# Two layers of a hybrid diffusion trunk: the beginning redone, a fourth load buffer, modulation sums closed two steps later

## Chip, cores and metric

One core of a Trainium2 chip. The time is the device time of one execution in microseconds; the kernel before was run three times: 1830.18, 1832.28 and 1832.47 us, median 1832.28. A separate execution was profiled: 1824.12 us, with a span of 1822.3 us from the first to the last instruction.

## The reference, cut to what matters

256 latent tokens `x` and 256 context tokens `ctx`, each of 1024 features, go through two layers. Every sub-layer normalises its input, scales and shifts it by vectors that a linear map makes from a condition (`c` for latent tokens, `c_ctx` for context tokens), and gates its output.

```python
def sandwich_in(x, mods, idx, g_pre):
    shift, scale = mods[3 * idx], mods[3 * idx + 1]
    return rms_norm(x, g_pre) * (1 + scale) + shift

def swiglu(h, w1, w2):
    a, b = jnp.split(h @ w1, 2, axis=-1)
    return (jax.nn.silu(a) * b) @ w2

    silu_c, silu_cc = jax.nn.silu(c), jax.nn.silu(c_ctx)
    for layer in range(DEPTH):
        m_lat = split(silu_c @ w_ada[layer] + b_ada[layer], 9)
        m_ctx = split(silu_cc @ w_ada[layer] + b_ada[layer], 9)
        # half-step SwiGLU, token mixing (three groups of heads), half-step SwiGLU
```

`w_ada` is 1024 x 9216 per layer, `ffn_w1` 1024 x 5632 and `ffn_w2` 2816 x 1024 per feed-forward. All is in 32-bit floating point.

## The kernel before

Activations lie feature-major: HH and HL hold, for each of the 8 tiles of 128 features, the high and the low part of 512 token columns (context 0 to 255, latent 256 to 511). Each product of 32-bit numbers is three matmuls, high by high, high by low and low by high. Weights come as units of mostly 512 KB: SyncE loads one into a buffer of the ring `raws` (three buffers), ScalarE casts it into the high part of a slot (line 186), VectorE subtracts to get the low part (line 191), and the buffer is free again. A unit for the modulation vectors of later sub-layers (`ada_v`, lines 446 to 491) isn't split: VectorE multiplies its rows by the condition and adds them up in SX (lines 464, 466), four units to a half of a block; then a step `red` sums over the partitions with four matmuls and copies the result into `rows` on ScalarE (line 474), and a step `fin` transposes `rows` (line 482) and adds biases (`mod_done`), or, for a gate, works on rows of GROW and writes them out (`gate_done`). For gates, `gate_rows` reads bias and norm rows into GROW (lines 432, 433) ahead of the four units.

The order of the work is written as lists of steps. `schedule` merges a main list with side steps that have due points (`spread` puts the modulation steps evenly into a feed-forward body); `run` walks the merged list and, before each step, issues loads as long as the buffer that the load needs has been freed, and splits as slots come free. The framework below then orders each engine's instructions by readiness in its own model of time, so an instruction may stand earlier in its engine's queue than its step. Every engine works its queue in order, SyncE's loads included.

The beginning. `start` asks for x, the two conditions (element by element into `csrc`, lines 1169 and 1170), constants and ctx. `x_stat` normalises the tokens of a group into GTB (lines 1186, 1191); `load_x` transposes all 8 feature tiles of the group and copies them from PSUM banks to YB (lines 1201, 1202). The first sub-layer's shift and scale are made tile by tile: `ada_k` multiplies the condition `sc` by two 512 KB blocks of `w_ada` (32 small matmuls), copies the sums into `rows` (line 1216), transposes (line 1221) and adds bias and gain. The blocks of tile 0 lie in `raws`, the others in three own buffers, the two halves of GTB and a part of SX, which are free only when the tokens have left GTB. `pre_one` scales and shifts one tile of one group (lines 1234 to 1236) into HH and HL, and `first_k` runs that tile's 18 matmuls of 512 columns for the first three pairs of hidden tiles, while later tiles are still being made. The order is pre_one(k), ada_k(k+2), first_k(k).

The buffer R holds split weights (XS slots), hidden activations (U), and in the mixing stage attention buffers, at overlapping addresses.

Of the kernel before, what the change touches and what calls it, by code (L numbers as in the profile page):

```python
# [16 lines left out]
P = 128  # L17
D = 1024
# [61 lines left out]
def hybrid_trunk(ctx: ExitStack, tc, x, c, ctx_in, c_ctx, w_ada, b_ada, norm_g, ffn_w1, ffn_w2, w_in, w_out,  # L80
# [36 lines left out]
    raws = [tile(f"raw{i}", [1024]) for i in range(3)]  # L117
# [10 lines left out]
    JUNK = tile("junk", [D], mybir.dt.bfloat16)  # L128
# [8 lines left out]
    U_HI = [R[:, i * 1024 : i * 1024 + T] for i in range(NU)]  # L137
    U_LO = [R[:, i * 1024 + T : (i + 1) * 1024] for i in range(NU)]
    XS = [R[:, 9216 + i * 2048 : 9216 + (i + 1) * 2048].rearrange("p (a n) -> p a n", a=2) for i in range(5)]
# [25 lines left out]
    class Unit:  # L165


        def __init__(self, src, split=True, slots=(0, 1, 2), lo=V):
            self.src, self.split, self.slots, self.lo_eng = src, split, slots, lo
            self.nk, self.n = src.shape[0] // P, src.shape[1]  # L170
            self.first = self.last = self.own = self.own_prev = None
            self.after, self.hi_v, self.tail = -1, False, False
# [33 lines left out]
    class Step:  # L206


        def __init__(self, fn, units=(), dur=0.0, after=(), needs=(), low=False):
            self.fn, self.units, self.dur, self.after, self.needs = fn, list(units), dur, list(after), list(needs)  # L210
            self.low = low
# [46 lines left out]
    def run():  # L258
# [108 lines left out]
    csrc = tile("csrc", [KD, 2])  # L367
# [9 lines left out]
    def layer_consts(l):  # L377
        ng, ba = S1(), S1()
        nc.scalar.dma_start(out=ng[0:48, 0:P], in_=norm_g[l].rearrange("a (k p) -> (a k) p", p=P))
        nc.scalar.dma_start(out=ba[0:72, 0:P], in_=b_ada[l].rearrange("(k p) -> k p", p=P))  # L380
        pt = XB()
# [66 lines left out]
    def ada_v(l, *js):  # L448

        st = []  # L450
        for j in js:
            for h in range(2):
                box = {}
                if j % 3 == 2:
                    st.append(Step(lambda l=l, j=j, h=h: gate_rows(l, j, h)))
                for q in range(4):
                    u = Unit(w_ada[l, q * SEQ : (q + 1) * SEQ, j * D + h * T : j * D + (h + 1) * T], split=False)
# [32 lines left out]
                st += [Step(red, dur=0.43), Step(fin, dur=0.0 if j % 3 == 2 else 0.22)]  # L490
        return st
# [20 lines left out]
    def tok_end(g, t, o, partial):  # L512
# [3 lines left out]
        for hf, c_ in enumerate(HALVES):  # L516
            if partial:
                V.tensor_tensor(out=y[:, c_], in0=o[hf], in1=y[:, c_], op=ALU.add)
            S.activation(out=JUNK[:, :T], in_=y[:, c_] if partial else o[hf], func=AF.Square, scale=RMS, accum_out=st[:, hf : hf + 1])
# [3 lines left out]
        for hf, c_ in enumerate(HALVES):  # L523
            V.scalar_tensor_tensor(out=x[:, c_], in0=S2T[:, c_], scalar=r, in1=x[:, c_], op0=ALU.mult, op1=ALU.add)  # L524
            S.activation(out=JUNK[:, :T], in_=x[:, c_], func=AF.Square, scale=RMS, accum_out=st[:, 2 + hf : 3 + hf])
# [27 lines left out]
    def out_end(t, o):  # L553

        st, x, gy = SR(), X[:, 2 + t], (S2T, SX[:, :D])[t]
        for hf in range(2):
            S.activation(out=JUNK[:, :T], in_=o[hf], func=AF.Square, scale=RMS, accum_out=st[:, hf : hf + 1])
# [604 lines left out]
    def start():  # L1162
# [6 lines left out]
        nc.scalar.dma_start(out=csrc[:, :, 0], in_=c_ctx.rearrange("(k p) -> p k", p=P))  # L1169
        nc.scalar.dma_start(out=csrc[:, :, 1], in_=c.rearrange("o (k p) -> p (o k)", p=P))  # L1170
        nc.sync.dma_start(out=cst[:, 0 : 3 * P], in_=const[:, 0 : 3 * P])
        for t in range(2):
            nc.sync.dma_start(out=xs[CTXG][:, t], in_=ctx_in[0, t * P : (t + 1) * P])
        S.activation(out=sc[:, 0, 0:1], in_=eps, func=AF.Silu)

    start()
    BX = Ring(banks[0:4] + banks[6:8])

    def start_late():
        nc.sync.dma_start(out=cst[:, 3 * P :], in_=const[:, 3 * P :])  # L1180

    def x_stat(g):

        st = SR()
        for t in range(2):
            S.activation(out=JUNK, in_=xs[g][:, t], func=AF.Square, scale=RMS, accum_out=st[:, t : t + 1])
        if g == LAT:
            S.activation(out=sc[:, :, 0:2], in_=csrc, func=AF.Silu)
        for t in range(2):
# [3 lines left out]
    def by_feature(g, ks):  # L1193
        return YB.rearrange("p g n -> p (g n)").rearrange("p (k t) -> p k t", k=KD)[:, ks, GROUPS[g]]

    def load_x(g):
        for kk in range(0, KD, 2):
            pt = BX().rearrange("p (k t) -> p k t", k=2)
            for z in range(2):
                for t in range(2):  # L1200
                    nc.tensor.transpose(out=pt[:, z, t * P : (t + 1) * P], in_=GTB[:, t, (kk + z) * P : (kk + z + 1) * P], identity=ident)
            V.tensor_copy(out=by_feature(g, slice(kk, kk + 2)), in_=pt)
# [28 lines left out]
    def pre_one(k, g):  # L1231
        gs = GROUPS[g]
        t = S2()[:, :SEQ]
        V.tensor_scalar(out=t, in0=by_feature(g, k), scalar1=A[0][:, 0, k, g : g + 1], scalar2=MOD[0][:, k, g : g + 1], op0=ALU.mult, op1=ALU.add)
        S.copy(out=HH[:, k, gs], in_=t)
        V.tensor_tensor(out=HL[:, k, gs], in0=t, in1=HH[:, k, gs].bitcast(F32), op=ALU.subtract)
# [23 lines left out]
    both = (LAT, CTXG)  # L1260
# [8 lines left out]
    consts0 = Step(lambda: layer_consts(0))  # L1269
    lx = {g: Step(lambda g=g: load_x(g), dur=1.7) for g in both}  # L1270
    flat = [u for us in ada0[1:] for u in us]
    for i, u in enumerate(flat):
        u.own, u.own_prev = raw_u[i % 3], flat[i - 3] if i >= 3 else consts0 if i == 2 else lx[CTXG]
    rs = {g: Step(lambda g=g: x_stat(g), dur=0.43) for g in both}
    pre = {(k, g): Step(lambda k=k, g=g: pre_one(k, g)) for k in range(KD) for g in both}
# [82 lines left out]
```

## Time and profile before

| | |
|---|---|
| median of three runs | 1832.28 us |
| profiled execution | 1824.12 us, span 1822.3 us |
| TensorE matmul busy | 1750.3 us, 96% |
| TensorE weight load busy | 1452.9 us, 80% |
| VectorE, ScalarE, GpSimd busy | 1170.7, 714.8, 72.8 us |
| read from memory | 257.51 MB, 142 GB/s over the span |
| mean granted TensorE clock | 0.987 of full |

Busy shares are means over stages with different limits. A group's idle time says what its engine waited for just before it; matmuls are pipelined, so a busy TensorE is not one at its peak. PE is TensorE's matmul, PEld its weight load, DVE VectorE, ACT ScalarE, POOL GpSimd, SPq the queue of SyncE.

### The profile page before, as it was taken

How to read it: one execution, taken by the hardware profiler on the slowest of the kernel's cores; microseconds unless marked ns; L12 is line 12 of the kernel's file. 1: busy time of each engine (PE TensorE's matmuls, PEld its weight loads, DVE VectorE, ACT ScalarE, POOL GpSimd, SP SyncE). 2: the span in 40 equal slices, each digit the busy share in tenths (PEclk: the TensorE clock that was granted, in tenths of full speed). 3: DMA queues.
4: the chain of work that ended last, by engine and by line, in shares of the span. 5: the costliest groups of instructions: out<-in, count | busy, mean ns of one | idle time of the engine just before them, and what ended most of it. 6: DMA issues, size and time to landing. Idle time of an engine off the chain costs nothing.

```text
span 1822.3 us, 24374 instructions
## 1 busy us (share of the span) xinstructions
PE 1750.3 (96%) x9496; PEld 1452.9 (80%) x9496; DVE 1170.7 (64%) x1889; ACT 714.8 (39%) x1244; POOL 72.8 (4%) x128
## 2 busy tenths in 40 slices
PE   4999999999999999999999999999999999969998
PEld 3788777778977779878878798888887897859997
DVE  4756776667367875757758565666765737865553
ACT  3323222235267763323222442322223526654442
POOL 0000000001000400000000000000000100200000
PEclk8999999999999999999999999999999999979999
DMA  7836555554211152656545334645554431255662
GB/s 230 243 116 192 176 173 157 167 171 125 57 47 47 64 171 71 188 163 182 176 148 176 124 105 127 197 122 183 176 161 156 115 69 58 93 151 187 187 187 76
DMA packets 301187, 260.19 MB, mean 143 GB/s; under 512 B 18064, under 2 KB 246160, under 8 KB 301072
## 3 DMA queue, kind: packets, MB, share of 16 engines
q1 hardware_dynamic: 297216, 257.67, 46.5%
q8 instruction: 74, 1.21, 0.3%
q10 hardware_dynamic: 3856, 0.97, 0.2%
q14 instruction: 41, 0.34, 0.1%
HBM read 257.51 MB, written 1.10 MB: 142 GB/s over the span
## 4 chain that ended last, share of the span: by engine, by line
PE 65%; DMA 14%; DVE 12%; ACT 5%; issue 3%; POOL 1%; SPq 0%; ACTq 0%; DVEq 0%; POOLq 0%
PE bank L90 62%; DMA raw<-in_ffn_w_dram 10%; DVE sx L466 3%; DVE R L191 2%; ACT R L186 2%; DVE w L191 2%; DMA raw<-in_w_ada_dram 2%; ACT w L186 1%; DMA gtb<-in_w_ada_dram 1%; POOL sr L507 1%; PE bank L802 1%; PE bank L536 1%; DMA csrc<-in_c_dram 1%; DVE sx L464 0%; DVE X L524 0%
## 5 line engine op out<-in xcount | busy, mean ns | idle before, releaser
L90 PE MATMUL bank<-HH,R 128*128 128x512 f32 (+1 forms) x2028 | 531.7, 347 | 4.7 <-ACT R L186 2.5
L90 PE MATMUL bank<-HH,w 128*128 128x512 f32 (+1 forms) x1540 | 433.9, 359 | 0.4 <-DVE w L191 0.4
L90 PEld LDWEIGHTS bank<-HH,R 128*128 128x128 f32 x2028 | 356.3, 191 | 59.5 <-issue 7.2
L90 PE MATMUL bank<-R 128*128 128x512 f32 (+3 forms) x1632 | 364.1, 376 | 2.9 <-DVE YB L642 1.1
L90 PE MATMUL bank<-HL,R 128*128 128x512 f32 (+1 forms) x1014 | 349.5, 345 | 0.0
L90 PEld LDWEIGHTS bank<-R 128*128 128x128 f32 (+1 forms) x1632 | 278.5, 188 | 74.0 <-issue 9.7
L191 DVE TENSOR_TENSOR R<-raw,R 128x1024 fp32r<-128x1024 f32 (+1 forms) x177 | 214.7, 1216 | 173.5 <-ACT R L186 170.1
L466 DVE SCALAR_TENSOR_TENSOR sx<-raw,sc,sx 128x512 f32<-128x512 f32 x448 | 310.8, 745 | 21.8 <-DMA raw<-in_w_ada_dram 21.4
L186 ACT CAST R<-raw 128x1024 fp32r<-128x1024 f32 (+1 forms) x177 | 184.3, 1043 | 343.3 <-DMA raw<-in_ffn_w_dram 270.3
L90 PEld LDWEIGHTS bank<-HH,w 128*128 128x128 f32 x1540 | 274.1, 190 | 50.2 <-issue 12.0
L191 DVE TENSOR_TENSOR w<-raw,w 128x1024 fp32r<-128x1024 f32 (+1 forms) x153 | 187.5, 1226 | 161.8 <-ACT w L186 161.5
L90 PE MATMUL bank<-HL,w 128*128 128x512 f32 (+1 forms) x770 | 274.7, 357 | 0.0
L186 ACT CAST w<-raw 128x1024 fp32r<-128x1024 f32 (+1 forms) x153 | 159.9, 1046 | 279.8 <-DMA raw<-in_ffn_w_dram 199.6
L90 PE MATMUL bank<-w,R 128*128 128x512 f32 x960 | 236.0, 396 | 2.6 <-ACT R L1008 1.8
L90 PEld LDWEIGHTS bank<-w,R 128*128 128x128 f32 x960 | 178.1, 189 | 43.4 <-ACT R L1008 2.3
L90 PEld LDWEIGHTS bank<-HL,R 128*128 128x128 f32 x1014 | 193.3, 191 | 22.4 <-DVE HL L541 0.2
L90 PEld LDWEIGHTS bank<-HL,w 128*128 128x128 f32 x770 | 146.5, 190 | 20.6 <-issue 2.3
L591 DVE TENSOR_TENSOR sil<-sil,bank 128x512 f32<-128x512 f32 (+1 forms) x96 | 55.5, 578 | 77.9 <-PE bank L90 77.7
L593 ACT CAST R<-sil 128x512 fp32r<-128x512 f32 (+1 forms) x96 | 51.2, 533 | 135.0 <-DVE sil L591 135.0
L507 POOL TENSOR_TENSOR sr<-sr,eps 128x1 f32<-128x1 f32 x42 | 28.3, 674 | 1463.5 <-DVE sr L506 1444.5
L590 ACT ACTIVATE sil<-bank 128x512 f32<-128x512 f32 (+1 forms) x96 | 48.9, 510 | 90.7 <-PE bank L90 84.4
L360 DVE TENSOR_TENSOR R<-bank,R 128x512 fp32r<-128x512 f32 (+2 forms) x86 | 47.9, 561 | 33.8 <-ACT R L359 33.5
(145 smaller groups left out, 1211.8 us busy)
## 6 DMA issues: line engine op xcount, KB each, us to landing
raw<-in_ffn_w_dram SPq DMA_DIRECT2D x258, 512.0 KB
raw<-in_w_ada_dram SPq DMA_DIRECT2D x130, 512.0 KB
raw<-in_w_in_dram SPq DMA_DIRECT2D x40, 512.0 KB
raw<-in_w_out_dram SPq DMA_DIRECT2D x24, 512.0 KB
gtb<-in_w_ada_dram SPq DMA_DIRECT2D x10, 512.0 KB
gtb<-gate SPq DMA_DIRECT2D x10, 512.0 KB
raw<-in_ffn_w_dram SPq DMA_DIRECT2D x8, 384.0 KB
sx<-in_w_ada_dram SPq DMA_DIRECT2D x4, 512.0 KB
```

The source lines that it names most:

```text
L90: return nc.tensor.matmul(out=o, lhsT=l, rhs=r, start=start, stop=stop)
L186: ins = S.copy(out=self.hi, in_=self.raw)
L191: ins = self.lo_eng.tensor_tensor(out=self.lo, in0=self.raw, in1=self.hi.bitcast(F32), op=ALU.subtract)
L360: V.tensor_tensor(out=lo, in0=src, in1=hi.bitcast(F32), op=ALU.subtract)
L466: V.scalar_tensor_tensor(out=ACC[v], in0=u.raw[:, z, :], scalar=sv, in1=ACC[v], op0=ALU.mult, op1=ALU.add)
L507: G.tensor_tensor(out=a, in0=a, in1=mhalf, op=ALU.pow)
L536: nc.tensor.transpose(out=pt[:, z, t * P : (t + 1) * P], in_=y[:, t, k * P : (k + 1) * P], identity=ident)
L590: S.activation(out=sl[:, cs], in_=oa, func=AF.Silu)
L591: V.tensor_tensor(out=sl[:, cs], in0=sl[:, cs], in1=ob, op=ALU.mult)
L593: tab["hs"] = S.copy(out=uh[:, cs], in_=sl[:, cs])
L802: nc.tensor.transpose(out=b[:, n * P : (n + 1) * P], in_=e[:, n * P : (n + 1) * P], identity=ident)
```

## The change

The conditions are loaded as 16 rows of 128 values, put through Silu, transposed once and copied into `sc` (`conditions`); the norm gains and biases of layer 0 are asked for at the start into the buffers `sil`, as are the condition rows. The context tokens are asked for after the blocks of tile 0; the first rows of w1 wait for a mark behind that. `x_stat` writes normalised tokens to YB instead of GTB, in half-row statistics; `load_x` is gone, and `pre_k` transposes one feature tile of both groups into one bank, scales from the bank and casts and subtracts over 512 columns. GTB and the part of SX are free for modulation blocks from the start. `raws` has four buffers; `junk` is halved, `csrc` gone. XS and U have other addresses in R. In `ada_v` `gate_rows` stands behind two of the four load steps, and `take` puts the step `fin` of each half block behind the first two steps of the next one.

```diff
-    raws = [tile(f"raw{i}", [1024]) for i in range(3)]
+    raws = [tile(f"raw{i}", [1024]) for i in range(4)]
-    U_HI = [R[:, i * 1024 : i * 1024 + T] for i in range(NU)]
+    U_AT = [i * 1024 for i in range(8)] + [19456]
+    U_HI = [R[:, i : i + T] for i in U_AT]
-    XS = [R[:, 9216 + i * 2048 : 9216 + (i + 1) * 2048].rearrange("p (a n) -> p a n", a=2) for i in range(5)]
+    XS = [R[:, 8192 + i * 2048 : 8192 + (i + 1) * 2048].rearrange("p (a n) -> p a n", a=2) for i in range(5)]
...
         def can_load(i):
-            if nl >= len(seq):
+            if nl >= len(seq) or mark.get(seq[nl].gate, -1) > i:
                 return False
             if seq[nl].own is not None:
                 p = seq[nl].own_prev
-                return (p.last if isinstance(p, Unit) else prog.index(p)) < i
+                return p is None or p.last < i
...
-                if j % 3 == 2:
-                    st.append(Step(lambda l=l, j=j, h=h: gate_rows(l, j, h)))
                 for q in range(4):
+                    if q == 2 and j % 3 == 2:
+                        st.append(Step(lambda l=l, j=j, h=h: gate_rows(l, j, h)))
...
                 st += [Step(red, dur=0.43), Step(fin, dur=0.0 if j % 3 == 2 else 0.22)]
+                st[-1].fin = True
...
-        nc.scalar.dma_start(out=csrc[:, :, 0], in_=c_ctx.rearrange("(k p) -> p k", p=P))
-        nc.scalar.dma_start(out=csrc[:, :, 1], in_=c.rearrange("o (k p) -> p (o k)", p=P))
+        nc.scalar.dma_start(out=CROW[0:KD, 0:P], in_=c_ctx.rearrange("(k p) -> k p", p=P))
+        nc.scalar.dma_start(out=CROW[KD : 2 * KD, 0:P], in_=c.rearrange("o (k p) -> (o k) p", p=P))
+        consts_load(0, *CSRC)
...
+    def conditions():
+        S.activation(out=CROW[0 : 2 * KD], in_=CROW[0 : 2 * KD], func=AF.Silu)
+        pt = XB()
+        nc.tensor.transpose(out=pt[:, 0 : 2 * KD], in_=CROW[0 : 2 * KD], identity=ident[0 : 2 * KD, 0 : 2 * KD])
+        V.tensor_copy(out=sc[:, :, 0:2].rearrange("p k v -> p v k"), in_=pt[:, 0 : 2 * KD].rearrange("p (v k) -> p v k", v=2))
...
         for t in range(2):
-            root(st, t)
-            V.tensor_scalar(out=GTB[:, t], in0=xs[g][:, t], scalar1=st[:, t : t + 1], scalar2=None, op0=ALU.mult)
+            for hf, c_ in enumerate(HALVES):
+                S.activation(out=JUNK, in_=xs[g][:, t, c_], func=AF.Square, scale=RMS, accum_out=st[:, 2 * t + hf : 2 * t + hf + 1])
+            V.tensor_scalar(out=y_of(g)[:, t], in0=xs[g][:, t], scalar1=root(st, 2 * t, 2 * t + 1), scalar2=None, op0=ALU.mult)
...
+    def pre_k(k):
+        pt, f = BS(), S2()
+        for g in both:
+            for t in range(2):
+                nc.tensor.transpose(out=pt[:, (2 * g + t) * P : (2 * g + t + 1) * P], in_=y_of(g)[:, t, k * P : (k + 1) * P], identity=ident)
+        for g in both:
+            V.tensor_scalar(out=f[:, GROUPS[g]], in0=pt[:, GROUPS[g]], scalar1=A[0][:, 0, k, g : g + 1], scalar2=MOD[0][:, k, g : g + 1], op0=ALU.mult, op1=ALU.add)
+        S.copy(out=HH[:, k], in_=f)
+        V.tensor_tensor(out=HL[:, k], in0=f, in1=HH[:, k].bitcast(F32), op=ALU.subtract)
...
+    main = [marked("ffn00"), Step(lambda: None, ada0[0]), Step(start_ctx), marked("ctx"), Step(lambda: None, [ku[0]])]
+    ku[0].gate = "ctx"
+    main += [Step(lambda: x_stat(LAT)), Step(conditions, dur=0.2), Step(lambda: layer_consts(0, CSRC), dur=0.2), Step(lambda: x_stat(CTXG))]
+    main += aks[0][0] + [aks[0][1]] + aks[1][0] + [aks[1][1]]
     for k in range(KD):
+        main.append(Step(lambda k=k: pre_k(k), dur=0.44))
+        if k + 2 < KD:
+            main += aks[k + 2][0] + [aks[k + 2][1]]
         main += first_k(k, ku[k], ALLC, f[3])
...
+            for s in f(*pieces.pop(0)):
+                if s.fin:
+                    late = [s, 2]
+                    continue
+                o.append(s)
+                if late:
+                    late[1] -= 1
+                    if not late[1]:
+                        o.append(late[0])
+                        late = []
+        return o + late[:1]
```

## Rows read from the trace of the kernel before

**Rows 1.** Windows: busy us (instructions) of each engine, granted clock, DMA share, GB/s.
```profile
0.00:31.10 31.10, 8.78 (x84) 6.97 (x84) 13.85 (x31) 10.62 (x18) 3.43 (x12) 0.94 0.72 212
31.10:67.00 35.90, 33.50 (x314) 24.12 (x310) 20.57 (x53) 12.41 (x25) 0.00 (x0) 0.91 1.02 282
...
79.40:430.00 350.60, 343.00 (x1555) 272.32 (x1554) 233.76 (x354) 100.94 (x144) 3.42 (x7) 0.99 0.51 158
```

**Rows 2.** Chain of waits in the first 80 us: start us, us, what.
```profile
1.24 9.32 DMA csrc<-in_c_dram
...
11.40 4.96 DMA subg<-in_diff_subln_g_dram
...
59.68 6.73 DMA gtb<-in_w_ada_dram
```

**Rows 3.** Timeline of SyncE's queue: start us, us, line, what it issues.
```profile
10.74 1.00 SPq L179 DMA_DIRECT2D raw<-in_w_ada_dram  x2
...
25.29 1.20 SPq L179 DMA_DIRECT2D gtb<-in_w_ada_dram  x2
```

**Rows 4.** Windows of 2 us in the beginning (columns as in rows 1).
```profile
4.00:6.00 2.00, 0.00 (x0) 0.00 (x0) 0.00 (x0) 0.00 (x0) 0.00 (x0) 1.00 0.92 261
6.00:8.00 2.00, 0.00 (x0) 0.00 (x0) 0.00 (x0) 0.00 (x0) 0.00 (x0) 1.00 1.06 372
...
20.00:22.00 2.00, 1.93 (x37) 1.36 (x35) 2.00 (x4) 0.00 (x0) 0.00 (x0) 1.00 0.00 0
...
30.00:32.00 2.00, 1.81 (x17) 0.88 (x17) 1.17 (x3) 0.07 (x1) 0.00 (x0) 0.50 1.13 322
```

**Rows 5.** Timeline of TensorE: start us, us, line, instruction, count.
```profile
23.84 1.53 PE L1201 MATMUL bank<-cst,gtb 128*128 128x128 f32 x12 [0.52 <-DVE gtb L1191]
...
31.11 0.80 PE L90 MATMUL bank<-HH,w 128*128 128x512 f32 x1
...
47.09 1.08 PE L90 MATMUL bank<-gtb,sc 128*32 128x128 f32 x32
...
52.65 0.65 PE L90 MATMUL bank<-sx,sc 128*32 128x128 f32 x16
...
67.02 0.50 PE L90 MATMUL bank<-HH,R 128*128 128x512 f32 x1
...
79.40 0.39 PE L90 MATMUL bank<-HH,R 128*128 128x512 f32 x1
```

**Rows 6.** Lines by form, 0 to 80 us: busy us, mean ns, idle before.
```profile
L1236 DVE TENSOR_TENSOR HL<-s,HH 128x256 fp32r<-128x256 f32 x16 | 6.1, 420 | 1.8 <-ACT HH L1235 1.5
L1234 DVE TENSOR_SCALAR s<-YB,A,mod 128x256 f32<-128x256 f32 x16 | 5.9, 410 | 0.2
...
L1202 DVE COPY YB<-bank 128x512 f32<-128x512 f32 x8 | 5.0, 686 | 0.8 <-PE bank L1201 0.8
...
L1191 DVE TENSOR_SCALAR gtb<-X,sr 128x1024 f32<-128x1024 f32 x4 | 2.9, 750 | 0.0
...
L593 ACT CAST R<-sil 128x512 fp32r<-128x512 f32 x2 | 1.2, 618 | 0.4 <-DVE sil L591 0.4
```

**Rows 7.** Waits of TensorE's weight loader, 80 us to the end: total, times, longest.
```profile
PEld bank L482 <- ACT rows L474: 7.3, 6, 3.1
```

**Rows 8.** Timeline of the weight loader: first and last of six such waits.
```profile
227.59 0.30 PEld L90 LDWEIGHTS bank<-HH,w 128*128 128x128 f32 x2 [0.79 <-DVE w L191]
...
356.46 0.50 PEld L90 LDWEIGHTS bank<-HH,R 128*128 128x128 f32 x2 [0.77 <-DVE R L191]
```

**Rows 9.** Windows behind three long holes (columns as in rows 1).
```profile
236.00:240.00 4.00, 3.63 (x11) 3.00 (x12) 3.93 (x9) 0.81 (x3) 0.00 (x0) 0.60 0.37 117
...
815.00:820.00 5.00, 4.26 (x13) 3.40 (x14) 4.57 (x8) 1.17 (x3) 0.00 (x0) 0.66 0.46 133
...
356.00:360.00 4.00, 3.95 (x15) 2.60 (x14) 1.01 (x2) 0.17 (x1) 0.00 (x0) 0.67 0.66 215
```

**Rows 10.** Waits of SyncE's queue: total us, times, longest.
```profile
SPq L179 <- DVE w L191: 373.1, 103, 19.4
```

More of the change, by code (lines that the diff above doesn't have):

```diff
@@ L127, in hybrid_trunk @@
     GROW = tile("grow", [3, SEQ])
-    JUNK = tile("junk", [D], mybir.dt.bfloat16)
+    JUNK = tile("junk", [T], mybir.dt.bfloat16)
     SR = Ring([tile(f"sr{i}", [6]) for i in range(8)])
@@ L136, in hybrid_trunk @@
     NU = 9
-    U_HI = [R[:, i * 1024 : i * 1024 + T] for i in range(NU)]
-    U_LO = [R[:, i * 1024 + T : (i + 1) * 1024] for i in range(NU)]
-    XS = [R[:, 9216 + i * 2048 : 9216 + (i + 1) * 2048].rearrange("p (a n) -> p a n", a=2) for i in range(5)]
+    U_AT = [i * 1024 for i in range(8)] + [19456]
+    U_HI = [R[:, i : i + T] for i in U_AT]
+    U_LO = [R[:, i + T : i + 1024] for i in U_AT]
+    XS = [R[:, 8192 + i * 2048 : 8192 + (i + 1) * 2048].rearrange("p (a n) -> p a n", a=2) for i in range(5)]
     MX = [R[:, i * 2048 : (i + 1) * 2048].rearrange("p (a n) -> p a n", a=2) for i in range(5)]
@@ L171, in __init__ @@
             self.first = self.last = self.own = self.own_prev = None
-            self.after, self.hi_v, self.tail = -1, False, False
+            self.after, self.hi_v, self.tail, self.gate = -1, False, False, None
         def view(self, t):
@@ L210, in __init__ @@
             self.fn, self.units, self.dur, self.after, self.needs = fn, list(units), dur, list(after), list(needs)
-            self.low = low
+            self.low, self.fin = low, False
             self.t = None
@@ L366, in hybrid_trunk @@
     sc = tile("sc", [KD, 32])
-    csrc = tile("csrc", [KD, 2])
     MOD = [tile(f"mod{l}", [9 * KD, 2]) for l in range(DEPTH)]
@@ L375, in hybrid_trunk, with consts_load, layer_consts @@
     LAM_INIT = [0.8 - 0.6 * math.exp(-0.3 * l) for l in range(DEPTH)]
-    def layer_consts(l):
-        ng, ba = S1(), S1()
+    def consts_load(l, ng, ba):
         nc.scalar.dma_start(out=ng[0:48, 0:P], in_=norm_g[l].rearrange("a (k p) -> (a k) p", p=P))
         nc.scalar.dma_start(out=ba[0:72, 0:P], in_=b_ada[l].rearrange("(k p) -> k p", p=P))
+    def layer_consts(l, src=None):
+        ng, ba = src or (S1(), S1())
+        if not src:
+            consts_load(l, ng, ba)
         pt = XB()
@@ L556, in out_end @@
         for hf in range(2):
[L557 removed]
+            S.activation(out=JUNK, in_=o[hf], func=AF.Square, scale=RMS, accum_out=st[:, hf : hf + 1])
             V.tensor_tensor(out=gy[:, hf * T : (hf + 1) * T], in0=o[hf], in1=GTB[:, LAT, hf * T : (hf + 1) * T], op=ALU.mult)
@@ L1185, in x_stat @@
         for t in range(2):
[L1186 to L1189, printed above, removed]
-            root(st, t)
-            V.tensor_scalar(out=GTB[:, t], in0=xs[g][:, t], scalar1=st[:, t : t + 1], scalar2=None, op0=ALU.mult)
[L1193 to L1202, printed above, removed]
+            for hf, c_ in enumerate(HALVES):
+                S.activation(out=JUNK, in_=xs[g][:, t, c_], func=AF.Square, scale=RMS, accum_out=st[:, 2 * t + hf : 2 * t + hf + 1])
+            V.tensor_scalar(out=y_of(g)[:, t], in0=xs[g][:, t], scalar1=root(st, 2 * t, 2 * t + 1), scalar2=None, op0=ALU.mult)
+    both = (LAT, CTXG)
     PAIRS = 3
@@ L1287, in take @@
     def take(n, f=ada_v):
-        o = []
+        o, late = [], []
         for _ in range(n):
-            o += f(*pieces.pop(0))
-        return o
+            for s in f(*pieces.pop(0)):
[9 more added lines that the diff above has]
+        return o + late[:1]
     body = f[1]
```

28 lines of the change are left out of this document (7 added, 21 removed).

## The prediction

> **What bounds the kernel now.** First the busy time by stage. From 79.4 us on TensorE is the bound: 343.0 of 350.6 us in the first long stage, with the DMA at 0.51. [...]
>
> Second, the chain of waits in the beginning. It starts with 9.32 us for the conditioning vector, read element by element, then 4.96 us in which VectorE stands before a small operand of the later mixing (`subg`), then loads into the modulation block buffers; the last of these still costs 6.73 us at 59.68 [rows 2]. Third, the queue of SyncE: the first weight load leaves at 10.74, and the first two loads into GTB at 25.29, because GTB holds the normalised tokens until they are transposed [rows 3]. The 2 us windows show the price: 261 and 372 GB/s while inputs come, nothing at 20 to 22 us, 322 GB/s once all buffers are open [rows 4]. Fourth, TensorE in order of time: first dense matmul at 31.11, the last of the eight feature tiles at 79.40 + 0.23 = 79.6, that is 48.5 us for a stage whose steady tile takes 52.65 - 47.09 = 5.56 us, and whose last three tiles (no modulation matmuls among them) take (79.6 - 67.0) / 3 = 4.2 us [rows 5].
>
> Fifth, the holes in the body. TensorE's weight loader waits 7.3 us, 6 times, for the copy `rows` before the transposes of a modulation sum [rows 7], and six times between 227 and 357 us for a split weight, in the two feed-forward parts of the first body: 6.6 us (0.79 in the first, 0.77 in the last) [rows 8]. After the longer holes the granted clock falls: 0.60, 0.67 and 0.66 in the windows behind three of them [rows 9]. Both kinds hang on the ring of three load buffers: SyncE waits 373 us, 103 times, for the VectorE split that frees one [rows 10], and the `rows` copy stands on ScalarE behind a cast that waits for such a load.
>
> **Conditions as rows; constants early.** Removed: the element-wise load of rows 2 (9.32 us) and with it ScalarE's wait in front of all statistics. Added: a Silu on 16 partitions, one small transpose, one copy, each below the 0.6 us of a full instruction, all before the inputs' statistics are done, so they cost nothing while the modulation weights are still coming. If that cover were gone they would cost under 1.5 us. What is late next is the data itself.
>
> **Own buffers, contexts after the first block.** The order on SyncE becomes x, constants, block 0 of the modulation weights, ctx, first w1 rows, then GTB, GTB and SX at once. In bytes: 1.25 MB of x and constants at 257 to 372 GB/s from 2 us on lands at 5.4 to 6.9 us; 1.05 MB of block 0 at 310 [an estimate just under the 322 of rows 4] at 8.8 to 10.3; ctx at 11.6 to 13.1; 0.39 MB of w1 at 13 to 14.4; block 1 at 16.3 to 17.8; the second half of block 2, which needs a buffer back, at 20 to 21. The statistics, now in halves of 512 columns (ScalarE takes 0.62 for a cast of that size [rows 6]), end beside these loads. The first dense matmul stands behind the modulation matmuls of block 2 in program order, but in the trace of before it began at 31.11 between them. So it can start between 16 (block 1 alone is waited for) and 23 us (block 2 and a cold chain); I take 19, in the middle, 12 us earlier than now.
>
> **Tokens turned tile by tile.** Removed: 32 transposes and eight VectorE copies of 0.69 us (5.0 us) ahead of the stage [rows 6]. Added on TensorE inside the stage: 4 transposes a tile, 12 of which take 1.53 us now [rows 5], so 0.5 us, with a turn-around 0.6, times 8 = 4.8 us on the path. Added as a wait: each tile's first matmul now needs transposes (0.5), two scalings on VectorE (2 x 0.41), one cast of 512 columns (0.62), 1.95 us in all, and the subtraction for HL 0.7 more [rows 6]; behind it on TensorE's in-order queue stand that tile's 18 matmuls, and VectorE may hold a weight split in front. Bounds: 0 where the transposes of the next tile slip between the matmuls of this one, 2.6 x 8 = 21 us where nothing hides it. I take 0.4 a tile, 3.2 us, nearer to the lower end, because modulation matmuls (1.36 us a tile, 5.56 - 4.2) stand between chain and use for six of eight tiles.
>
> [...]
>
> Sum of the stage: start 19; 8 x 4.2 matmuls = 33.6; transposes 4.8; modulation matmuls of blocks 2 to 7, 6 x 1.36 = 8.2; low clock 3.2 (0.09 of 35.9 us in rows 1, kept, since the first work still comes after a pause); chain 3.2; DMA 1, since 1.44 MB a tile at 310 GB/s is 4.7 us against 6.2 of TensorE. End at 73.0 instead of 79.6: 6.6, or **7 us**. The same sum for the kernel as it is, 33.6 + 7 x 1.36 + 3.2 = 46.3, leaves 2.2 of the measured 48.5 for waits on the DMA. Best case (16, no chain, no DMA) 65.8, a gain of 14; worst (23, chain 21, DMA 4) 97.8, a loss of 18.
>
> **Modulation sums finished two steps later.** The `rows` copy then has two load steps more; 7.3 us of holes [rows 7] and 3.3 of clock behind the two long ones [rows 9] can go, 10.6 in all; late next is the weight that was hidden behind the hole. Rows for the gates are read after two load steps instead of before: the same four DMAs behind the same wait; taken at nothing, at worst a load late by some us once per gate.
>
> **Fourth load buffer.** One more load in flight. It can take away the six weight holes, 6.6 us, and 1.3 of clock [rows 8, 9], 7.9; at worst it puts loads of the body ahead of modulation blocks in the beginning, 0.52 MB at 310 GB/s = 1.7 us. The holes of the tails and of mixing are bound to marks, not to this ring, and stay. Together with the part above the limits are 18.5 and -2; I take **13 us**, as closing a hole lets TensorE reach the next late load sooner. The moved addresses of R (XS, U) change which buffers overlap at the stage borders, where TensorE waits for the norms: 0, within 2 us either way.
>
> **Sum.** 7 + 13 = 20 us off the profiled execution's own 1824.1 (span 1822.3): 1804. The median of the runs, 1832.3, lies 8 above it; I take the 20 off that: **1812**.
>
> **Rivals.** (a) Only the beginning gains, the holes return as the next late load: 1832 - 7 = 1825. For it: ScalarE's cast still waits in order for each load. Against: SyncE waits for buffers, not the DMA, which is half idle. (b) Only the body gains: the beginning is paced by the DMA or the chain: 1832 - 13 = 1819. For it: 1.02 DMA share in rows 1. (c) Everything at its best: 14 + 18.5 off, 1799. (d) The other side: the chain of each tile is bare and the clock falls behind it, as after the holes of rows 9 (1.6 each): stage 19 + 33.6 + 4.8 + 8.2 + 3.2 + 1 + 8 x (2.6 + 1.6) = 103.4, 24 lost, against 13 gained: 1843. It decides once a tile loses over (6.6 + 3.2 + 13) / 8 = 2.9 us. Against it: the chain alone is 2.6. (e) Nothing reachable moves, each step only shifts its wait: 1832.
>
> **Chances.** Forecast 0.45, (a) 0.17, (b) 0.17, (c) 0.09, (d) 0.06, (e) 0.06. A difference under 0.2%, 3.7 us, can't be told from none. Faster: forecast, (a), (b), (c), less 0.04 for a part of (a) that ends within that bound: 0.84; same 0.09; slower 0.07. The forecast's own range is 1803 to 1822; for 8 in 10, with (a) and (b) inside and most of (c), 1799 to 1829.
>
> **What would show it.** Right: the first load of modulation weights leaves before 4 us and GTB's before 10; no empty 2 us window before 25; first 512-column matmul at 16 to 23 and the eighth tile over by 66 to 78; `rows` no longer among what the weight loader waits for; no weight hole over 1 us from 200 to 360. Wrong: holes over 1 us in front of most tiles ended by the scalings or the casts; a granted clock of half the rate past 35 us; the same 13 us of holes under other names.

## The result, and the profile after

The changed kernel takes 1807.75 us (median of 4 runs, 1806.32 to 1811.6) against 1832.12 for the kernel before (4 runs, 1830.18 to 1832.47): ratio 0.9872, interval 0.9855 to 0.989, 24.4 us off. The forecast was 1812. Later, in sets of runs that took both kernels on one chip, it was 1808.37 against 1824.62 (6 and 17 runs; ratio 0.991, interval 0.9893 to 0.9926), 16.3 us off: the changed kernel repeats, the kernel before was 1824.6 to 1826.4 in all four later sets. So the number that the experiments have to explain is 16, and where the other 8 of the first set lie is a question of its own (first experiment).

The profiled execution of after takes 1808.16 us with a span of 1806.4, 15.9 less than before's 1822.3. The end of the eighth feature tile cuts this in two: it ends at 77.29 us, before at 79.63 [rows 5], so in this pair of profiles **the beginning gave 2.3 us and everything behind it 13.6**. That is not the 7 and 13 of the forecast.

Windows of after, over the same stretches as [rows 1] and two of [rows 4] (busy us of PE, PEld, DVE, ACT, POOL; granted clock; DMA share; GB/s):

```profile
0.00:31.10 31.10, 14.93 (x163) 10.40 (x163) 10.15 (x29) 11.00 (x26) 3.88 (x12) 1.00 0.95 279
31.10:67.00 35.90, 31.10 (x243) 24.21 (x244) 23.81 (x49) 13.61 (x20) 0.00 (x0) 0.90 0.94 273
79.40:430.00 350.60, 346.55 (x1617) 278.81 (x1616) 242.28 (x367) 108.83 (x160) 5.17 (x9) 1.00 0.54 161
...
6.00:8.00 2.00, 0.83 (x3) 0.54 (x3) 0.54 (x4) 1.51 (x5) 0.55 (x1) 1.00 1.11 318
20.00:22.00 2.00, 2.00 (x18) 1.64 (x22) 1.01 (x4) 0.00 (x0) 0.00 (x0) 1.00 0.82 211
```

The first 31 us are better used: the DMA share is 0.95 instead of 0.72, no window of 2 us before 31 is without loads, and TensorE is busy for 14.9 us instead of 8.8. The third row shows the gain of the body: 62 more matmuls in the same 350.6 us. The second row is the surprise: between 31.1 and 67 us TensorE is busy for 2.4 us less than before, and its clock is no better.

The chain of waits in after's beginning, and the queue of SyncE [rows 2, 3] (start us, us, what):

```profile
1.38 3.68 DMA sil<-in_c_dram
...
5.21 5.60 DMA subg<-in_diff_subln_g_dram
...
11.27 7.02 DMA gtb<-in_w_ada_dram
...
22.93 5.66 DMA raw<-in_ffn_w_dram
...
39.90 7.07 DMA raw<-in_ffn_w_dram
```

```profile
2.10 2.57 SPq L181 DMA_DIRECT2D raw<-in_w_ada_dram  x2
...
10.83 1.02 SPq L181 DMA_DIRECT2D gtb<-in_w_ada_dram  x2
```

Read as rows, the conditions land in 3.68 us instead of 9.32; the modulation weights leave at 2.10 instead of 10.74, GTB's blocks at 10.83 instead of 25.29. The load of the small operand `subg` is still in the chain (5.60 us, before 4.96), and GTB's blocks leave behind it. The chain now goes over two loads of first-layer rows for a feature tile (22.93 and 39.90), which were not in it before.

TensorE of after in order of time, the first and last of what matters [rows 5] (in brackets: idle time before it and what ended that):

```profile
23.25 0.74 PE L90 MATMUL bank<-HH,w 128*128 128x512 f32 x2 [0.34 <-ACT HH L1244]
...
31.50 0.41 PE L1226 MATMUL bank<-cst,rows 128*128 128x128 f32 x2 [2.18 <-DVE s L1243]
...
38.10 1.08 PE L90 MATMUL bank<-gtb,sc 128*32 128x128 f32 x32
39.91 0.73 PE L90 MATMUL bank<-HH,w 128*128 128x512 f32 x2 [0.73 <-ACT HH L1244]
...
48.39 0.73 PE L90 MATMUL bank<-HH,R 128*128 128x512 f32 x2 [2.40 <-ACT HH L1244]
...
56.79 0.73 PE L90 MATMUL bank<-HH,R 128*128 128x512 f32 x2 [0.73 <-ACT HH L1244]
...
63.79 1.09 PE L1241 MATMUL bank<-cst,YB 128*128 128x128 f32 x7
64.88 1.21 PE L90 MATMUL bank<-HH,R 128*128 128x512 f32 x4
...
77.29 0.39 PE L90 MATMUL bank<-HH,w 128*128 128x512 f32 x1
```

The first dense matmul comes at 23.25 instead of 31.11, 7.9 us earlier, and 5.5 of these are lost again on the way to 77.29. In front of tiles 1 to 4 stands a hole, and three of the four are ended by the cast of that tile (HH). The transposes of the last two tiles (seven of the eight in the row at 63.79) stand ahead of tile 5's matmuls, and from there on no hole is left: three tiles in 77.29 - 64.88 = 12.4 us, 4.1 each. That is a hint inside the trace: tiles that were turned ahead cost their matmuls and nothing else, like the last three of the kernel before, 4.2 each, whose tokens had all been turned long before.

Two of these holes change the clock too, and the windows behind the former long holes of the body are clean now [rows 9]:

```profile
32.00:36.00 4.00, 4.00 (x13) 3.08 (x11) 2.73 (x6) 1.47 (x3) 0.00 (x0) 0.58 1.04 297
48.00:52.00 4.00, 3.61 (x12) 2.92 (x13) 3.36 (x7) 2.71 (x4) 0.00 (x0) 0.71 1.17 291
...
236.00:240.00 4.00, 4.00 (x20) 3.24 (x19) 4.00 (x10) 1.68 (x2) 0.00 (x0) 1.00 0.60 190
356.00:360.00 4.00, 4.00 (x20) 3.31 (x19) 3.53 (x7) 0.60 (x1) 0.00 (x0) 1.00 0.65 227
815.00:820.00 5.00, 5.00 (x24) 4.14 (x23) 4.43 (x9) 0.36 (x1) 0.00 (x0) 1.00 0.59 178
```

What the weight loader of after waits for from 80 us to the end (total us, times, longest) [rows 7]; the wait for `rows`, 7.3 us before, is no longer among its rows:

```profile
PEld bank L90 <- ACT R L188: 3.7, 5, 1.1
PEld bank L90 <- ACT w L188: 3.3, 4, 1.5
```

The two rows are waits for the cast of a weight, 7.7 and 2.5 us in the kernel before.

### The profile page after: what moved, and what is told of

The parts are those of the page before. It is cut to its first block, busy times and chain, and to the rows that moved or that the text cites. A ratio compares the mean times of both kernels' runs of the same rounds, so it can differ in the third digit from the quotient of the medians.

```text
span 1806.4 us, 24364 instructions
## 1 busy us (share of the span) xinstructions
PE 1742.6 (96%) x9497; PEld 1449.9 (80%) x9497; DVE 1166.3 (65%) x1874; ACT 714.7 (40%) x1244; POOL 75.5 (4%) x128
## 4 chain that ended last, share of the span: by engine, by line
PE 77%; DMA 8%; DVE 8%; ACT 4%; issue 2%; POOL 1%; ACTq 0%; DVEq 0%; SPq 0%; POOLq 0%
PE bank L90 75%; DMA raw<-in_ffn_w_dram 7%; DVE w L193 2%; DVE R L193 1%; ACT R L188 1%; POOL sr L513 1%; PE bank L808 1%; ACT w L188 1%; PE bank L542 1%; DVE sx L471 1%; DVE s L527 1%; DVE YB L532 0%; DVE X L530 0%; DMA raw<-in_w_ada_dram 0%; ACT junk L531 0%
## 5 line engine op out<-in xcount | busy, mean ns | idle before, releaser
L90 PEld LDWEIGHTS bank<-w,R 128*128 128x128 f32 x960 | 177.4, 188 | 44.2 <-DVE YB L648 2.1
```

The source lines that it names most:

```text
L90: return nc.tensor.matmul(out=o, lhsT=l, rhs=r, start=start, stop=stop)
```

## The experiments

The stage from the first dense matmul to the end of the eighth tile decides most of them. This table is worked out from one row of windows for each profile (the rows that verdicts rest on stand below): the stage ends where the first matmul behind the eighth tile starts, idle is length less TensorE's busy time, low clock is length times what the mean granted clock lacks of 1.

| kernel | stage starts | length | idle | low clock | ends |
|---|---|---|---|---|---|
| before | 31.11 | 48.52 | 2.4 | 3.4 | 79.63 |
| before, again | 31.10 | 46.78 | 2.1 | 1.4 | 77.88 |
| body alone | 31.00 | 47.50 | 1.4 | 3.3 | 78.50 |
| beginning alone | 23.31 | 55.51 | 7.6 | 3.3 | 78.82 |
| after | 23.25 | 54.04 | 6.6 | 3.2 | 77.29 |
| after, again | 23.16 | 53.20 | 6.3 | 1.6 | 76.36 |
| after, tiles turned ahead | 23.06 | 47.56 | 2.6 | 0.0 | 70.62 |
| beginning alone, tiles turned ahead | 23.09 | 48.03 | 2.1 | 0.0 | 71.12 |

Each line is one execution. The two pairs of the same kernel show the scatter: 0.3 us of idle time, but some 2 us of low clock and 1 to 2 us at the end. The granted clock on record also misses some slow stretches (last section), so the column of idle time is the one to go by.

**The kernel before once more**, unchanged.

> The kernel before, unchanged, profiled once more. Its profiled execution (1824.1 us) was 8 us under the median of its runs (1832.1). Theory A: the 8 us are holes of TensorE, and stretches at the lower clock level behind them, that come and go between executions; then another profile shows 1830 to 1832 us, a mean clock under 0.987, and more low-clock stretches in the body after 80 us. Theory B: they lie in the first 80 us, which change with how the first transfers land; then the first tiles end later than 79.6 us by most of the 8.

Measured: 1825.35 (8 runs) against 1825.82 (22 runs of the same kernel), ratio 0.9997 (0.9981 to 1.0013). The profiled execution takes 1825.82 and lies inside the other runs, which is what neither theory had. So a profiled execution isn't 8 us faster than a timed one: the first set of the kernel before was slower than every later one, by 6 to 8 us in the median. Why, these runs don't show; the later sets ran on four chips, and the chip of the first set isn't on record, so that another chip is to blame is neither shown nor excluded. Like for like the change is worth 16 us, and that is what the parts below have to add up to.

**The body alone**: four load buffers, and both moves of the modulation steps (sums finished two steps later, gate rows read later), on the old beginning (room for the buffer comes from a smaller scratch tile; the squares of the statistics go to GTB, which is free then).

```diff
-    raws = [tile(f"raw{i}", [1024]) for i in range(3)]
+    raws = [tile(f"raw{i}", [1024]) for i in range(4)]
...
-                if j % 3 == 2:
-                    st.append(Step(lambda l=l, j=j, h=h: gate_rows(l, j, h)))
                 for q in range(4):
+                    if q == 2 and j % 3 == 2:
+                        st.append(Step(lambda l=l, j=j, h=h: gate_rows(l, j, h)))
...
+                st[-1].fin = True
...
+                if s.fin:
+                    late = [s, 2]
+                    continue
...
```

> The kernel before with only the two body parts of the change: four load buffers, and the modulation sums finished two steps later with the gate rows read later; the beginning is as before. Theory A (the body holds most of the gain): 13 us off, as the two traces differ after the eighth tile, up to 21 where the 8 us between profile and runs are holes of the same kind: 1811 to 1819 us. Theory B (the beginning holds most of it): not under 1825.

Measured: 1809.96 (4 runs) against 1825.82, ratio 0.9917 (0.9897 to 0.9938), 15.9 off, as theory A had it. The eighth tile ends at 78.5, between the two profiles of before. All that the change gives like for like, this part gives.

**Its two halves.** The two moves alone (the last three pieces of the diff above), and the fourth buffer alone (its first piece).

> The kernel before with only the modulation sums finished two steps later and the gate rows read later, three load buffers. If the 7.3 us of waits for `rows` and 3.3 us of low clock behind them go by this alone: 8 to 11 us off, 1821 to 1824. If the fourth buffer is what empties ScalarE's queue and this edit alone only shifts the hole to the next late weight: within 3 us of 1832.

Measured: 1819.10 (11 runs), ratio 0.9963 (0.9951 to 0.9974), 6.7 off, a little under the 8 to 11 expected.

> The kernel before with only a fourth load buffer (the statistics write their unused squares to GTB, to make room). If weights come one load earlier and the six weight holes and the clock behind them go: 6 to 8 us off, 1824 to 1826; if it also takes the `rows` holes, since the cast in front of the copy then waits less: 13 or more, under 1819. If loads only wait elsewhere: within 3 us of 1832.

Measured: 1816.68 (6 runs), ratio 0.9947 (0.9928 to 0.9966), 9.1 off, between the two expectations. 6.7 + 9.1 = 15.8, the 15.9 of both. The weight loader's waits with the fourth buffer alone, 80 us to the end:

```profile
PEld bank L90 <- ACT R L186: 4.8, 5, 2.0
...
PEld bank L482 <- ACT rows L474: 2.1, 2, 1.4
```

The buffer alone takes 5.2 of the 7.3 us of `rows` waits, although nothing about these sums was moved. This fits the forecast's reading, that the copy stood on ScalarE behind a cast that waited for a load: before the longest of these waits (3.06 us at 236.37) the copy of 235.94 stands behind a cast that had waited 3.82 us for its load. The first row had 7.7 us in the kernel before. With the two moves alone the `rows` waits are gone too, but other weights are late at other places, as in these rows of that kernel (2.5 and 1.9 us in the kernel before):

```profile
PEld bank L90 <- ACT w L186: 6.0, 9, 2.4
...
PEld bank L90 <- DVE w L191: 3.5, 7, 1.0
```

**The changed kernel once more**, unchanged: 1808.37 (6 runs; ratio above), its eighth tile ends at 76.36. Its 16.3 us are 0.4 more than the body alone gave, less than either theory had.

> The changed kernel, unchanged, beside the variants of it. The four load buffers and later sums alone took 15.9 us off (0.9917 of the kernel before). Theory A, from the traces (eighth tile over at 77.3 us instead of 79.6): the beginning adds 2 to 3 us, 0.990. Theory B, from the prediction: it adds 7, 0.988.

**The beginning alone**: the changed kernel with three load buffers, and with sums and gate rows where the kernel before has them.

```diff
-    raws = [tile(f"raw{i}", [1024]) for i in range(4)]
+    raws = [tile(f"raw{i}", [1024]) for i in range(3)]
...
+                if j % 3 == 2:
+                    st.append(Step(lambda l=l, j=j, h=h: gate_rows(l, j, h)))
...
-            for s in f(*pieces.pop(0)):
-                if s.fin:
...
+            o += f(*pieces.pop(0))
+        return o
```

> The changed kernel with three load buffers and with the sums and gate rows of before: the new beginning and the new addresses in R alone. Theory A: 2 to 3 us off the kernel before, ratio 0.998 to 0.999. Theory B (the forecast's term): 7 us off, 0.996. Rival: a slower beginning, as the chain of each tile is bare and three buffers hold the w1 rows up more than four: over 1.000.

Measured: 1824.59 (12 runs) against 1824.62, ratio 0.9998 (0.9987 to 1.0009): nothing. The forecast's 7 us fall with this run, and so do the 2 to 3 that the trace seemed to leave. Three rows say why, the stage of the kernel before (first profile, then run again), and of the beginning alone:

```profile
31.11:79.63 48.52, 46.12 (x370) 34.54 (x367) 32.10 (x73) 17.70 (x34) 0.00 (x0) 0.93 0.94 267
```

```profile
31.10:77.88 46.78, 44.68 (x371) 33.51 (x368) 31.96 (x72) 17.80 (x34) 0.00 (x0) 0.97 0.96 276
```

```profile
23.31:78.82 55.51, 47.90 (x346) 37.68 (x347) 36.85 (x68) 19.05 (x29) 0.00 (x0) 0.94 0.85 245
```

It starts 7.8 us earlier. Against the second row it is 8.7 longer: 5.5 of idle time, 1.9 of clock, 1.3 of work (the transposes that moved in, less the modulation matmuls that moved out). Against the first it is 7.0 longer, 5.2 of idle time and 1.8 of work; the clock is the same. So idle time is what eats the start, and the clock's part lies within the scatter of two profiles.

**First-layer rows asked for one tile earlier**, on the changed kernel: the chain goes over these loads, so perhaps they are the cause.

```diff
         main.append(Step(lambda k=k: pre_k(k), dur=0.44))
+        if k + 1 < KD:
+            main.append(Step(lambda: None, [ku[k + 1]]))
```

> The changed kernel with the w1 rows of each feature tile asked for one tile earlier. Theory A: the holes of 2.4 to 2.7 us in front of tiles 1 and 3 (31.5 and 48.4 us) and the half-clock stretches behind them come from the cast of late w1 rows that stands on ScalarE and VectorE ahead of the tile's own scaling and cast; asked for earlier they go: 4 to 9 us off the changed kernel. Rival B: the DMA engines are full there, so earlier rows only make the modulation blocks late: within 2 us, or slower, with holes ended by the loads into GTB and SX.

Measured: 1810.45 (6 runs) against 1824.62, ratio 0.9917 (0.9901 to 0.9932): no gain over 1808.37, and theory A falls for this load. The hole at 31 is gone, but the one before tile 3 has grown from 2.40 to 3.30 us. ScalarE of this kernel shows what stands there:

```profile
47.53 1.04 ACT L188 CAST w<-raw 128x1024 fp32r<-128x1024 f32 x1 [6.07 <-DMA raw<-in_ffn_w_dram]
48.48 0.61 ACT L1244 CAST HH<-s 128x512 fp32r<-128x512 f32 x1
```

A weight of the body (1024 columns) has taken the place of the tile's rows in front of the cast, and it waited 6.07 us for its load. The late rows choose the place of a hole; they are not its only cause.

The eighth tile ends at 82.18, but that mark can't be set beside 77.29 as it is: 12 later matmuls of 512 columns stand in front of it here (360 matmuls in the stage, in after 345), 2.7 us at 0.23 each. And from its start to 28 us its matmuls of 512 columns followed each other every 0.43 us (26.21, 26.64, 27.07) instead of 0.23 (in after 24.28, 24.51, 24.74), by estimate another 2 us (some ten of them, 0.2 more each); the second profile of the changed kernel has such a stretch too, a shorter one, so the rows need not be its cause.

**Tile 0 turned before the second modulation block**, besides this: an earlier start.

```diff
-    main += aks[0][0] + [aks[0][1]] + aks[1][0] + [aks[1][1]]
+    main += aks[0][0] + [aks[0][1]] + [Step(lambda: pre_k(0), dur=0.44)] + aks[1][0] + [aks[1][1]]
...
-        main.append(Step(lambda k=k: pre_k(k), dur=0.44))
+        if k:
+            main.append(Step(lambda k=k: pre_k(k), dur=0.44))
```

> As the kernel with earlier w1 rows, and tile 0 of the tokens is turned ahead of the second modulation block's matmuls. Theory A: the first 512-column matmul, at 23.25 us in the changed kernel, waits for its place behind the modulation matmuls of blocks 1 and 2, not for data; it moves to about 20 us, and 2 to 4 us more come off than by earlier rows alone. Rival B: the stage is paced by the transfers, so an earlier first tile only waits longer for the second block: no further gain.

Measured: 1807.13 (6 runs), ratio 0.9904 (0.9889 to 0.992). The first dense matmul comes at 20.27, 3 us earlier, and the eighth tile ends at 78.04. Against its own base, the rows asked for earlier (1810.45 in the same set), it is 3.3 us faster in the median, which is what theory A expected, though the two intervals overlap; against the changed kernel (1808.37) it is 1.2, which can't be told from none. Whether an earlier start is kept in this order stays open.

**Loads of the body held behind the last modulation block**, on the changed kernel: in its trace SyncE issues weights of the body between the blocks and the rows, from 41.23 us on.

```diff
+                        if u not in ku and u not in ada0[0] and len(ring) < 24:
+                            behind(u.dma, flat[-1].dma)
```

> The changed kernel with the weight loads of the feed-forward body held behind the last modulation block on SyncE's queue (some 3 MB that now go ahead of it). Theory B (the transfers pace the tiles): modulation blocks land up to 8 us earlier and the eighth tile ends at 69 to 73. Theory A (the chain does): the eighth tile ends within 2 us of 77, and the body's first weights, asked for later, may cost some us: 0.991 or more of the kernel before.

Measured: 1810.41 (6 runs) against 1825.18, ratio 0.9918 (0.9899 to 0.9938): no gain, against theory B. Now the modulation sum and the tile behind it are late, with TensorE busy for 1.31 of 4 us while the DMA share is 1.03; on ScalarE the copy of that sum stands at 61.50 behind two casts of body weights that waited 4.49 and 1.07 us for their loads. The eighth tile ends at 81.58, again with 12 later matmuls of 512 columns in front. Windows of this kernel:

```profile
60.00:64.00 4.00, 1.31 (x8) 0.84 (x8) 3.46 (x6) 2.01 (x3) 0.00 (x0) 1.00 1.03 329
64.00:68.00 4.00, 3.08 (x7) 2.48 (x8) 3.10 (x7) 1.81 (x4) 0.00 (x0) 0.60 0.48 140
```

**Tiles turned ahead**, on the changed kernel: a tile's transposes, scalings and cast go behind the first group of matmuls of the tile before, so that the other two groups and the modulation matmuls cover its chain.

```diff
+    pres = [Step(lambda k=k: pre_k(k), dur=0.44) for k in range(KD)]
+    main.append(pres[0])
     for k in range(KD):
-        main.append(Step(lambda k=k: pre_k(k), dur=0.44))
...
-        main += first_k(k, ku[k], ALLC, f[3])
+        fk = first_k(k, ku[k], ALLC, f[3])
+        main += fk[:1] + pres[k + 1 : k + 2] + fk[1:]
```

> The changed kernel with each tile's tokens turned and scaled behind the first of the three matmul groups of the tile before, instead of behind the last. In the changed kernel the first matmul of tiles 0 to 5 comes every 8.3 us (23.25, 32.06, 39.91, 48.39, 56.79, 64.88), against 6.2 that its matmuls and transposes take; the prediction took 0.4 us a tile for the chain transposes, scaling, cast. Theory A (that chain stands bare, 1 us a tile and up to 2.7 with a late w1 row in front of the cast, and the clock falls behind the long ones): the holes ended by the HH cast go, the eighth tile ends at 68 to 71 us instead of 77, and the kernel is 6 to 9 us faster than the changed one, 0.986 to 0.988 of the kernel before. Theory B (the transfers pace the tiles, at 0.94 of the DMA engines): the holes come back in front of the modulation matmuls, ended by loads into GTB and SX, the eighth tile stays within 2 us of 77, and the ratio at 0.991.

Measured: 1800.36 (5 runs, 1798.74 to 1803.72) against 1825.18 (11 runs), ratio 0.9864 (0.9842 to 0.9885): 24.8 off, some 8 more than the changed kernel, as theory A had it. This is the version that beats both. Its windows and its TensorE in order of time:

```profile
23.06:70.62 47.56, 45.01 (x344) 34.23 (x345) 34.10 (x64) 20.63 (x30) 0.00 (x0) 1.00 0.98 286
...
36.00:40.00 4.00, 2.67 (x13) 1.75 (x14) 1.99 (x6) 1.85 (x3) 0.00 (x0) 1.00 1.06 321
40.00:44.00 4.00, 4.00 (x47) 3.03 (x46) 3.36 (x6) 1.46 (x2) 0.00 (x0) 1.00 1.12 314
```

```profile
39.03 0.44 PE L1226 MATMUL bank<-cst,rows 128*128 128x128 f32 x2 [1.02 <-ACT rows L1221]
...
51.59 0.60 PE L1241 MATMUL bank<-cst,YB 128*128 128x128 f32 x4
...
61.89 0.74 PE L90 MATMUL bank<-HH,R 128*128 128x512 f32 x2 [0.85 <-ACT HH L1244]
```

The four transposes of a tile (51.59) stand with no idle time before them between matmuls that are ready. Against the row of after

```profile
23.25:77.29 54.04, 47.46 (x345) 37.49 (x345) 35.79 (x66) 18.35 (x28) 0.00 (x0) 0.94 0.88 259
```

the stage is 6.5 us shorter: 4.0 of idle time and 3.2 of clock less, with work 0.8 the other way; against after's second profile it is 5.6, 3.7 of idle time and 1.6 of clock less. The DMA share has risen from 0.88 to 0.98, so the loads are likely the next limit.

**Tiles turned ahead and tile 0 before the second block**, both together.

```diff
-    main += aks[0][0] + [aks[0][1]] + aks[1][0] + [aks[1][1]]
+    main += aks[0][0] + [aks[0][1]]
+    pres = [Step(lambda k=k: pre_k(k), dur=0.44) for k in range(KD)]
+    main += [pres[0]] + aks[1][0] + [aks[1][1]]
```

> As the kernel with the tiles turned ahead, and tile 0 turned before the second modulation block, so that the first 512-column matmul comes at about 20 us. Theory A: 2 to 3 us faster than turning ahead alone, as the tiles then follow each other without holes. Theory B: no faster, the DMA engines being full; the tiles wait for their modulation blocks.

Measured: 1802.53 (6 runs), ratio 0.9872 (0.9852 to 0.9892), not to be told from the one above, as theory B had it. The start is at 20.17, the eighth tile ends at 73.75: with the start pulled ahead a modulation block is not there yet (a hole of 1.59 us at 30.24 ends with its load into SX), TensorE is busy for 1.29 us of the four from 28 on, and the clock of the next four is 0.59.

```profile
28.00:32.00 4.00, 1.29 (x33) 0.75 (x32) 0.69 (x1) 0.98 (x2) 0.00 (x0) 1.00 0.94 252
32.00:36.00 4.00, 3.85 (x13) 3.21 (x14) 1.53 (x4) 1.20 (x3) 0.00 (x0) 0.59 1.09 297
```

**The beginning alone, tiles turned ahead**: the diff of the tiles turned ahead, on the kernel of the beginning alone.

> The new beginning with three load buffers and sums finished and gate rows read where the kernel before has them (the beginning alone, which was worth 0.0 us), and each tile's transposes, scalings and cast placed behind the first group of matmuls of the tile before. Theory A (the new beginning's start, 8 us earlier, is real and was eaten by the bare chain between tiles; what the order gave on the whole change, 8 us, it gives on the beginning alone): about 8 us below the kernel before, ratio 0.9957 (0.994 to 0.997); the eighth tile ends at 70 to 73 us; the body stays as it is before, with the waits for rows near 7 us. Theory B (what the order gave needs the fourth load buffer, without which the loads that come earlier stand behind one another again): under 3 us below, ratio 0.9985 to 1.001, and the eighth tile ends at 75 us or later.

Measured: 1816.63 (6 runs) against 1826.39 (11 runs), ratio 0.9945 (0.993 to 0.9961): 9.8 off, of an expected 8. Its stage:

```profile
23.09:71.12 48.03, 45.91 (x346) 34.38 (x346) 34.58 (x65) 18.77 (x28) 0.00 (x0) 1.00 0.94 273
```

7.7 us earlier at its end than without the new order, with the waits for `rows` in the body still there (6.6 us). The start that the beginning wins is real; the order of the tiles decides whether it is kept. 9.8 here and 15.9 of the body make 25.7, against 24.8 measured for both.

## Why the prediction was right, and where it was not

**The time was right, in part by luck.** 20 us were forecast, 24.4 measured in the first set and 16.3 in the later one. The body was forecast at 13 and gave 13.6 in the trace and 15.9 alone; the beginning was forecast at 7 and gave 2.3 in the trace and 0.0 alone. The 20 were 4 more than was won like for like, and they were taken off a 1832 that no later set repeats (1824.6 to 1826.4); the two errors offset each other. What happened is rival (b), "only the body gains", with a body worth 3 us more than it said; its time, 1819, missed because it, too, took its gain off the 1832 of the first set.

**Two steps failed: the start ("I take 19, in the middle") and the chain ("I take 0.4 a tile, 3.2 us, nearer to the lower end").** In the forecast's own sum the start, 4.25 us late, is the whole miss at the end of the eighth tile (77.29 instead of 73.0); the chain's error is hidden there by the work. The experiments show that the chain's part can be won back.

**The chain.** The reason given for the small term was that modulation matmuls stand between a tile's chain and its use. They do, but they last 1.1 us (the row at 38.10), and two scalings and a cast 1.7 (2 x 0.54 and 0.62): tiles 2 and 4 stand bare for 0.73. In all, in after the casts of HH end 5.5 us of holes (five, the longest 2.7), another of 2.4 us stands before tile 1, and idle time is 6.6 us in all instead of 3.2 + 1. The weight loader's waits of after from 22.5 to 77.3 us:

```profile
PEld bank L90 <- ACT HH L1244: 5.5, 5, 2.7
PEld bank L1226 <- issue: 2.4, 1, 2.4
```

The time between the first matmuls of tiles 0 to 5 is (64.88 - 23.25) / 5 = 8.3 us, where the sum had 6.6 and 3.2 of clock once. The longest hole shows the part that the sum lacked: the cast waits its turn behind another instruction that waits. ScalarE of after, in order of time:

```profile
46.99 0.83 ACT L188 CAST R<-raw 128x768 fp32r<-128x768 f32 x1 [5.39 <-DMA raw<-in_ffn_w_dram]
47.72 0.61 ACT L1244 CAST HH<-s 128x512 fp32r<-128x512 f32 x1
```

The scalings of this tile were over at 46.0; its cast stood behind the split of a weight whose rows landed 7.07 us after 39.90. The forecast had named this for VectorE ("may hold a weight split in front") and not priced it on ScalarE. Both occur: before tile 1 the two scalings, from 30.36 on, stand on VectorE behind a split of 0.96 us, whose cast on ScalarE had waited for the load of 22.93. That turning a tile ahead takes away holes and 8 us is shown; that the rows' lateness alone is not the cause is shown by the run that asked for them earlier, where a body weight stood in their place. A kernel with the cast moved ahead of the split on ScalarE was not run.

**The start**: 19 forecast with 16 to 23 as bounds, 23.25 measured, just past the late bound; block 1 landed at 18.29 against 16.3 to 17.8, and behind it stood a sum, tile 0's chain and block 2. What it cost stays open: 3 us earlier gave nothing with the tiles turned ahead and, in the median, 3.3 us with the rows asked for earlier. Of the forecast's signs two were missed narrowly (this one, and GTB's loads, which left at 10.83 and not before 10), and one sign of being wrong came true, matmuls at a lower clock past 35 us (0.71 in 48 to 52). **The stage's length** was forecast at 54.0 and measured at 54.04, by offsetting errors: work 44.2 instead of 46.6, idle time 6.6 instead of 4.2, clock 3.2 as forecast, though not in the first work of the stage (1.00 from 23.25 to 32) but behind two holes (0.58 and 0.71).

**Conditions and constants at nothing**: not contradicted. They land at 5.06 us, while the loads run on (DMA share 1.11 at 6 to 8 us). **Buffers of their own**: loads earlier as forecast, no empty window.

**The scalings from a bank.** In after they take

```profile
L1243 DVE TENSOR_SCALAR s<-bank,A,mod 128x256 f32<-128x256 f32 x16 | 7.9, 538 | 7.9 <-PE bank L1241 7.9
```

538 ns on average instead of 410 from SBUF [rows 6], 0.13 us more each and 2.0 us for 16; the forecast's chain has 2 x 0.41. With the tiles turned ahead more of this lies under matmuls: in the stage the weight loader waits 2.2 us for the casts behind the scalings, in after 5.5.

**The body**: the waits for `rows` went, and no hole over 1 us ended by a weight is left between 200 and 360 us; one of 2.1 us at 273 remains, ended by the addition of partial outputs (L648). The shares were other than the sum's: 7.9 was put down to the buffer and 9.1 measured, 10.6 to the later sums and 6.7 measured. The buffer alone takes most of the `rows` waits as well, and the later sums alone leave other weights late; why the two still add up to the whole, these traces don't show. SyncE's wait for a free buffer did not shrink (after's row, against 373.1 in [rows 10]):

```profile
SPq L181 <- DVE w L193: 381.9, 103, 19.9
```

It waits as long for the fourth buffer as for the third. That wait was a sign of a full ring and no measure of what a larger one gives; the holes of TensorE, 7.3 and 6.6 us in the forecast's reading, came nearer. **Gate rows and moved addresses at nothing**: the gate rows were only run together with the later sums, so their share stays open; the addresses are part of the beginning alone, which is worth 0.0.

## What to carry to other kernels

An earlier start can be worth nothing where the stage behind it loses the time again (here 7.8 us earlier gave 0.0): work out the first and the last item of a stage, not only the first. When a preparation is cut into pieces and placed in front of each use, put piece k+1 behind the first part of the work on piece k; a chain over three engines in order (here 2 us of transposes, scalings and cast) needed more cover than its own length, since each engine may have something in front that waits. Before you set the end of a stage beside another kernel's, count the matmuls in both stages. And measure the kernel before in the same runs as its change: here it moved by 6 to 8 us between sets, up to a third of the effect.

## What the runs showed of the hardware

The granted clock fell behind idle stretches of 2.2 us (0.58 in the window 32 to 36, after) and of 2.4 us (0.71, 48 to 52), and matmuls of 512 columns then followed each other every 0.43 us (33.48, 33.91, 34.34) instead of 0.23 (24.28, 24.51, 24.74). So in that profile two holes of 4.6 us together cost some 3.2 us more.

The length of a hole alone does not decide it. With the tiles turned ahead the clock stayed at 1.00 behind holes of about 1 us (39.03). In the second profile of the changed kernel it stayed at 1.00 behind a hole of 2.09 us before 46.37, and fell behind two of 0.54 and 0.81 us that lie close together between 59 and 61:

```profile
46.00:50.00 4.00, 3.63 (x17) 3.00 (x18) 3.40 (x7) 2.69 (x4) 0.00 (x0) 1.00 1.14 289
58.00:62.00 4.00, 2.65 (x43) 1.84 (x42) 2.88 (x7) 1.60 (x3) 0.00 (x0) 1.00 1.08 309
62.00:66.00 4.00, 3.90 (x12) 2.89 (x11) 3.94 (x10) 2.62 (x4) 0.00 (x0) 0.57 0.22 84
```

The granted clock on record does not show every slow stretch either: with the rows asked for earlier, matmuls of 512 columns start at 26.21, 26.64 and 27.07, 0.43 us apart, in a window that reads 1.00. The pace of the matmuls is the surer sign.

```profile
24.00:28.00 4.00, 4.00 (x11) 3.12 (x12) 1.62 (x5) 1.10 (x2) 0.00 (x0) 1.00 1.14 313
```
